# Tap matrices of a depthwise convolution: built in the feed-forward network before it and fetched back from DRAM, with the modulation steps of the two convolution stages redistributed

## The chip, the core and the metric

The kernel runs on one core of a Trainium2 chip. A core has a matrix engine (TensorE, PE in the profile; its weight loads are a row of their own, PEld), a vector engine (VectorE, DVE), a scalar engine (ScalarE, ACT), a general engine (GpSimd, POOL) and a sync engine (SyncE, SP) that here issues nearly all DMA transfers. Each engine works through its own instructions in their written order and waits on semaphores for the others.

The metric is the device time of one launch in microseconds. The kernel before takes 2255.34 us (median of three runs, 2252.38 to 2259.39).

## The reference

A trunk of two layers over 256 positions of 2048 channels, fp32, with one conditioning vector `c`:

```python
for i in range(2):
    mod = silu(c) @ ada_w[i] + ada_b[i]          # 6 x 2048 modulation values
    sh_m, sc_m, gt_m, sh_f, sc_f, gt_f = split(mod, 6)
    h = x * (1 + sc_m) + sh_m
    y = s5_mixer(h) if i == 0 else conv_mixer(h)
    x = layer_norm(ALPHA * x + (1 + gt_m) * y)
    h = x * (1 + sc_f) + sh_f
    x = layer_norm(ALPHA * x + (1 + gt_f) * swiglu_ffn(h))     # hidden width 5632

def conv_mixer(u):
    ab = u @ w_pw1                                # 2048 x 4096
    v = ab[..., :d] * sigmoid(ab[..., d:])
    v = depthwise_causal_conv(v, w_dw, 31 taps) + b_dw
    return silu(layer_norm(v)) @ w_pw2            # 2048 x 2048
```

## The kernel before, in words

**Stages.** The S5 mixer and its gated projection (to about 395 us of the span), the feed-forward network of layer 0 (FFN0, about 420 to 1152), an entry panel (1152 to 1179) that starts the first pointwise product of the convolution while the layer norm behind FFN0 is finished, that product with the depthwise convolution (to about 1390), the second pointwise product pw2 (to about 1490), and the feed-forward network of layer 1 (FFN1, to about 2235).

**Weights.** They are streamed from DRAM once, in units. A load of SP (line 586) brings a unit into a tile `raw`; ACT rounds it to `whi` (line 860), DVE forms the rest `wlo = raw - whi` (line 861, 128x2048 elements), and PE multiplies (lines 931 and 935): 16 matmuls with `whi` and 8 with `wlo` for a unit. FFN0 has two parts: in each, first panels of four units from `w_gu` (gate and up projections), then units from `w_down`. Within a panel the gated product is made by ACT and DVE from PSUM (`fsg`, lines 1286 to 1288), turned by PE (`turned`, line 947) and split for the down product (line 952). The first pointwise product of the convolution has the same form with `sg` (line 1134).

**Modulation.** Two thirds of `silu(c) @ ada_w`, most of layer 1's and some of layer 0's, are not done as matmuls but as a queue of 128 steps (`AdaQueue`). A step is a 1 MB load `rawa` on SP (line 687) and a multiply-add `adaacc` over 128x2048 on DVE (line 702). When the steps of a part are all done, four matmuls `adar` and four transposes `adat` on PE add it up. A step is drawn once for each weight unit whenever a credit that grows by `ada.rate` reaches one, and none while `ada.hold` is set.

**Convolution.** Of 16 chunks of 128 channels some have their 31 taps summed on DVE (line 1732, from `pad` or `vpad`), and eleven go over PE: POOL multiplies a mask `fold` with the taps into a matrix `lw` (line 1646, 128x1024, three buffers), the padded chunk goes to DRAM (`scr<-pad`) and comes back shifted (`vs<-scr`), and 32 matmuls `conv<-vs,lw` (line 1769, 32x256) give the sums. What runs later than the unit it is called in is put in a list `later` with a number of units.

**Order.** A scheduler fixes each engine's instruction order when the program is built; `queue_behind` holds an instruction behind another of the same engine.

## Time and profile before

| | |
|---|---|
| runs | 2252.38, 2255.34, 2259.39 us |
| profiled execution | 2254.45 us, of which the span is 2252.4 us |
| granted TensorE clock | 0.995 |
| PE busy in the span | 2200.4 us (98%) |
| DVE | 1677.5 us (74%) |
| ACT | 1017.3 us (45%) |
| POOL | 155.4 us (7%) |
| DMA | 579.50 MB, mean 257 GB/s |

The span runs from the first to the last instruction of the profiled execution; 2.05 us of its time lie outside the span. A timeline row gives the start in the span, the duration, the engine, the line, the operation with the tile written and the tiles read, and in brackets the idle time before it with what ended it. Rows of the same kind that follow one another are merged, with their count.

### The profile page before, as it was taken

Reading aid. Unit: us, or ns where it says so; the run is one execution under the profiler, and the core shown is the slowest. Engines: PE = TensorE matmul, PEld = TensorE weight load, DVE = VectorE, ACT = ScalarE, POOL = GpSimd, SP = SyncE. Lnnn points to the kernel's source line nnn. Section 1 sums busy time; section 2 is a strip of 40 time slices with the busy share of each in tenths; the row PEclk is TensorE's granted clock in tenths of the full one; section 3 lists DMA queues with packets and bytes.
Section 4 is the critical chain, followed back from the end, with each engine's and each line's share of the span. In section 5 each row is a group of like instructions: output and inputs, shape, how many; then the busy total and the mean of one; then the engine's idle time right before and its main releaser. Section 6 shows DMA issues by size and latency. Waiting matters only on the chain.

```text
span 2252.4 us, 33443 instructions
## 1 busy us (share of the span) xinstructions
PE 2200.4 (98%) x13619; PEld 1795.8 (80%) x13619; DVE 1677.5 (74%) x1839; ACT 1017.3 (45%) x1234; POOL 155.4 (7%) x265
## 2 busy tenths in 40 slices
PE   6999999999999999999999999999999999999998
PEld 4556778888787888787897777898888888888888
DVE  8897998887777777777988979888755444555474
ACT  4775334644333333344455434566434333434343
POOL 5771000000000000000010010000000000000000
PEclk9999999999999999999999999999999999999999
DMA  9998999599999899999856686757865555555542
GB/s 333 346 324 281 326 347 303 184 321 319 325 321 329 322 319 323 319 326 323 301 178 189 212 217 231 274 187 236 279 222 186 194 194 189 187 189 187 187 166 96
DMA packets 382848, 579.50 MB, mean 257 GB/s; under 512 B 13923, under 2 KB 282355, under 8 KB 368227
## 3 DMA queue, kind: packets, MB, share of 16 engines
q1 hardware_dynamic: 382070, 576.82, 75.5%
q8 instruction: 107, 1.75, 0.3%
q0 software_dynamic: 384, 0.46, 0.1%
q14 instruction: 47, 0.39, 0.1%
q10 hardware_dynamic: 240, 0.08, 0.0%
HBM read 573.74 MB, written 3.57 MB: 256 GB/s over the span
## 4 chain that ended last, share of the span: by engine, by line
PE 80%; DVE 10%; DMA 4%; ACT 2%; issue 2%; SPq 1%; POOL 0%; POOLq 0%; DVEq 0%; ACTq 0%
PE acc L931 65%; PE acc L935 8%; DVE wlo L861 2%; DMA raw<-in_ffn_w_gu_dram 2%; PE acc L1043 2%; PE turned L947 2%; PE conv L1769 2%; ACT whi L860 1%; DVE adaacc L702 1%; DMA raw<-in_s_w_glu_dram 1%; DMA raw<-in_ada_w_dram 1%; DVE pin L476 1%; PE ada L630 1%; PE y L499 1%; PE adar L710 0%
## 5 line engine op out<-in xcount | busy, mean ns | idle before, releaser
L861 DVE TENSOR_TENSOR wlo<-raw,whi 128x2048 fp32r<-128x2048 f32 x343 | 786.6, 2294 | 451.6 <-ACT whi L860 448.3
L860 ACT CAST whi<-raw 128x2048 fp32r<-128x2048 f32 x343 | 653.8, 1906 | 794.6 <-PE acc L931 424.5
L931 PE MATMUL acc<-whi,h 128*128 128x512 f32 x3584 | 873.7, 393 | 4.2 <-ACT whi L860 4.0
L931 PEld LDWEIGHTS acc<-whi,h 128*128 128x128 f32 x3584 | 667.3, 188 | 151.0 <-ACT whi L860 7.1
L931 PE MATMUL acc<-wlo,h 128*128 128x512 f32 x1792 | 453.6, 390 | 1.9 <-DVE wlo L861 1.8
L931 PEld LDWEIGHTS acc<-wlo,h 128*128 128x128 f32 x1792 | 335.4, 188 | 73.5 <-DVE wlo L861 4.2
L931 PE MATMUL acc<-whi,f 128*128 128x512 f32 x1248 | 300.9, 391 | 0.0
L702 DVE SCALAR_TENSOR_TENSOR adaacc<-rawa,c_act,adaacc 128x2048 f32<-128x2048 f32 (+1 forms) x135 | 284.6, 2108 | 0.4
L931 PEld LDWEIGHTS acc<-whi,f 128*128 128x128 f32 x1248 | 232.8, 188 | 49.5 <-ACT whi L860 1.7
L931 PE MATMUL acc<-wlo,f 128*128 128x512 f32 x624 | 156.6, 389 | 0.0
L931 PEld LDWEIGHTS acc<-wlo,f 128*128 128x128 f32 x624 | 117.0, 188 | 24.6 <-DVE wlo L861 0.4
L1646 POOL TENSOR_TENSOR lw<-fold,wtap 128x1024 f32<-128x1024 f32 x11 | 24.0, 2187 | 1050.5 <-PE acc L935 860.0
L935 PE MATMUL acc<-h,whi 128*128 128x256 f32 x640 | 83.7, 285 | 0.8 <-DVE h L1843 0.8
L935 PEld LDWEIGHTS acc<-h,whi 128*128 128x128 f32 x640 | 79.0, 191 | 6.1 <-issue 4.2
L630 PE MATMUL ada<-raw,c_rep 128*32 128x512 f32 (+1 forms) x576 | 69.2, 564 | 7.1 <-DMA raw<-in_ada_w_dram 6.9
L1286 ACT ACTIVATE fsg<-acc 128x256 f32<-128x256 f32 x84 | 31.7, 380 | 96.8 <-PE acc L931 96.8
L1224 POOL CAST lnmh<-lno 128x2 fp32r<-128x2 f32 x1 | 0.2, 183 | 874.2 <-DVE lno L68 874.2
L1287 DVE TENSOR_TENSOR fsg<-acc,fsg 128x256 f32<-128x256 f32 x84 | 35.1, 420 | 18.2 <-ACT fsg L1286 18.1
L935 PE MATMUL acc<-h,wlo 128*128 128x256 f32 x320 | 43.0, 283 | 0.0
L935 PE MATMUL acc<-f,whi 128*128 128x256 f32 x320 | 40.8, 284 | 0.0
L935 PEld LDWEIGHTS acc<-h,wlo 128*128 128x128 f32 x320 | 40.4, 192 | 0.0
L935 PEld LDWEIGHTS acc<-f,whi 128*128 128x128 f32 x320 | 39.4, 192 | 0.2
(367 smaller groups left out, 1837.8 us busy)
## 6 DMA issues: line engine op xcount, KB each, us to landing
raw<-in_ffn_w_gu_dram SPq DMA_DIRECT2D x352, 512.0 KB, 4.7
rawa<-in_ada_w_dram SPq DMA_DIRECT2D x128, 1024.0 KB, 5.6
raw<-in_ffn_w_down_dram SPq DMA_DIRECT2D x88, 1024.0 KB, 5.1
raw<-in_ada_w_dram SPq DMA_DIRECT2D x64, 1024.0 KB, 7.5
raw<-in_cv_w_pw_dram SPq DMA_DIRECT2D x66, 512.0 KB, 5.0
raw<-in_s_w_glu_dram SPq DMA_DIRECT2D x64, 512.0 KB, 10.2
raw<-in_cv_w_pw_dram SPq DMA_DIRECT2D x15, 1024.0 KB, 5.4
vs<-scr SPq DMA_DIRECT2D x40, 142.0 KB, 4.8
```

The costliest lines, as they stand in the source:

```text
L630: nc.tensor.matmul(acc[32 * (k % 4):32 * (k % 4) + 32, :], c_rep[:, kk, :], r[:, k, :], start=kk < 4, stop=kk >= NCH - 4)
L702: nc.vector.scalar_tensor_tensor(out=acc, in0=r[:, i], scalar=c_act[:, kk:kk + 1], in1=acc, op0=MUL, op1=ADD)
L860: m1 = nc.scalar.copy(out=hi[:, ks], in_=r[:, ks])
L861: m2 = nc.vector.tensor_tensor(out=lo[:, ks], in0=r[:, ks], in1=hi[:, ks].bitcast(F32), op=SUB)
L931: nc.tensor.matmul(acc[bank].rearrange("p a b -> p (a b)"), x[:, bank * HALF:(bank + 1) * HALF], wt[:, k], start=first, stop=end)
L935: nc.tensor.matmul(acc[bank][:, i], wt[:, k, m * P:(m + 1) * P], x, start=first and i == 0, stop=end and i == len(banks[bank]) - 1)
L947: nc.tensor.transpose(b[:, o:o + HALF], u[t][:, c0 + k * P:c0 + (k + 1) * P], ident)
L1043: nc.tensor.matmul(acc[m][:, 0:EW], wt[:, k, m * P:(m + 1) * P], xx[:, 4 * u + k], start=u == 0 and n == 0, stop=u == 3 and n == len(order ...
L1286: nc.scalar.activation(out=t[:, i], in_=gv[:, 0], func=AF.Sigmoid)
L1287: nc.vector.tensor_tensor(out=t[:, i], in0=gv[:, 0], in1=t[:, i], op=MUL)
L1646: nc.gpsimd.tensor_tensor(out=lw, in0=fold32.unsqueeze(1).unsqueeze(1).broadcast_to([P, 4, CONV_G, 32]), in1=bc(wtap[:, :, 4 * c:4 * c + 4 ...
L1769: nc.tensor.matmul(acc[32 * q:32 * q + 32, :], lw[:, q, g, :], vs[:, q, 4 * g:4 * g + SEQ], start=g == 0, stop=g == n - 1)
```

## The change

**Tap matrices.** A new `taps_matrix(c, h)` makes half a chunk's matrix (128x512) on POOL, into a tile that shares its two buffers with the tag `hf`, and SP writes it (256 KB) to a DRAM tile, `lw_kept[c]`. It is put into FFN0's list `later` at units 50 to 106, 22 times (eleven chunks, two halves). In the convolution the POOL operation (128x1024) goes, and `kept_taps(c)` loads the 512 KB of a chunk from DRAM into `lw`, ahead of the `vs<-scr` copies. The DRAM pool now lives as long as the kernel.

**Modulation steps.** `ada.rate` is 0.5 instead of 0.25 in the convolution, and `ada.hold` is no longer lifted for pw2. The convolution draws seven steps instead of two, pw2 none instead of five; 128 in all, as before.

```diff
         ada.rate, ada.behind = 0.77, True
+        dramp = ctx.enter_context(tc.tile_pool(name="dram", bufs=1, space=bass.MemoryType.DRAM))
+        lw_kept = {c: dramp.tile([P, 4, CONV_G * 32], F32, name=f"lw{c}") for c in range(NCH) if c not in V_CHUNKS or c == 15}
+
+        def taps_matrix(c, h):
+
+            t = sp.tile([P, 2, SEQ], F32, tag="hf", name="lw", bufs=2)
+            with queue_behind(newest.marks):
+                nc.gpsimd.tensor_tensor(
+                    out=t.rearrange("p q (g c) -> p q g c", c=32), in0=fold32.unsqueeze(1).unsqueeze(1).broadcast_to([P, 2, CONV_G, 32]),
+                    in1=bc(wtap[:, :, 4 * c + 2 * h:4 * c + 2 * h + 2].rearrange("p g q -> p q g"), 3, 32), op=MUL)
+            nc.sync.dma_start(lw_kept[c][:, 2 * h:2 * h + 2], t)
+
+        for n, c in enumerate(lw_kept):
+            for h in range(2):
+                later.put(50 + (27 * (2 * n + h)) // 10, lambda c=c, h=h: taps_matrix(c, h))
         entry = ffn(0, mod[0][:, 5], stats, wp, sp, fp, entry, (cv_w_pw1[0], [(0, 256), (D, 256)]),
...
-        dramp = cvctx.enter_context(tc.tile_pool(name="dram", bufs=1, space=bass.MemoryType.DRAM))
...
-        ada.rate = 0.25
+        ada.rate = 0.5
...
-        def taps_matrix(c):
+        def kept_taps(c):
             lw = cp.tile([P, 4, CONV_G, 32], F32, tag="lw", name="lw", bufs=3)
-            nc.gpsimd.tensor_tensor(
-                out=lw, in0=fold32.unsqueeze(1).unsqueeze(1).broadcast_to([P, 4, CONV_G, 32]),
-                in1=bc(wtap[:, :, 4 * c:4 * c + 4].rearrange("p g q -> p q g"), 3, 32), op=MUL)
+            nc.sync.dma_start(lw.rearrange("p q g c -> p q (g c)"), lw_kept[c])
             return lw
...
+            lws = []
+
+            def back():
+                lws.extend(kept_taps(ch + k) for k in range(len(vs)))
+                conv_copies(scr[i], vs)
+
             if i == 6:
                 to_scratch()
-                later.put(1, lambda: conv_copies(scr[i], vs))
+                later.put(1, back)
             else:
                 later.put(wait - 3, to_scratch)
-                later.put(wait - 2, lambda: conv_copies(scr[i], vs))
+                later.put(wait - 2, back)
             for k, v in enumerate(vs):
-                lw = taps_matrix(ch + k)
-                later.put(wait + k, lambda k=k, v=v, lw=lw: conv_out(ch + k, v, lw))
+                later.put(wait + k, lambda k=k, v=v: conv_out(ch + k, v, lws[k]))
...
-            v, lw = cp.tile([P, 4, LS], F32, tag="vs", name="vs", bufs=3), taps_matrix(c)
+            v, lw = cp.tile([P, 4, LS], F32, tag="vs", name="vs", bufs=3), kept_taps(c)
...
-        ada.hold = False
         ada.finish(1, 2)
         stats = Stats("ln10", sp)
-        ada.rate, ada.credit = 1.0, 0.0
...
             if q == 3:
-                ada.hold = True
                 raw = entry_raw(fp)
...
-            ada.rate = 0.5
```

**Where the instructions land.** SP's instructions at the seam of FFN0's first part, where its loads go over from `w_gu` to `w_down`. Before:

```order
127 L586 DMA raw<-in_ffn_w_gu_dram 128x4x256 x2
128 L586 DMA raw<-in_ffn_w_down_dram 128x4x512
129 L687 DMA rawa<-in_ada_w_dram 128x2048
130 L586 DMA raw<-in_ffn_w_down_dram 128x4x512
131 L687 DMA rawa<-in_ada_w_dram 128x2048
132 L586 DMA raw<-in_ffn_w_down_dram 128x4x512
133 L687 DMA rawa<-in_ada_w_dram 128x2048
134 L586 DMA raw<-in_ffn_w_down_dram 128x4x512 x2
```

The changed kernel at the same place (`lw_4597<-lw` is a write of half a matrix to DRAM):

```order
131 L586 DMA raw<-in_ffn_w_gu_dram 128x4x256 x2
132 L1623 DMA lw_4596<-lw 128x512
133 L1623 DMA lw_4597<-lw 128x512
134 L586 DMA raw<-in_ffn_w_down_dram 128x4x512
135 L1623 DMA lw_4597<-lw 128x512
136 L1623 DMA lw_4598<-lw 128x512
137 L687 DMA rawa<-in_ada_w_dram 128x2048
138 L1623 DMA lw_4598<-lw 128x512
139 L1623 DMA lw_4599<-lw 128x512
140 L586 DMA raw<-in_ffn_w_down_dram 128x4x512
141 L1623 DMA lw_4599<-lw 128x512
142 L1623 DMA lw_4600<-lw 128x512
```

Here 17 of the 22 writes follow one another in pairs, each pair ahead of one load (a `w_down` unit and a `rawa` by turns at first, the last ones all ahead of `w_down` units), and the sixth `w_down` load is the first with none ahead of it but a `rawa`; the other five stand some 100 instructions earlier, near the third panel of that part. Each write waits for its POOL operation, and each POOL operation for the write two before it.

PE's instructions in a panel of FFN0's second part. Before:

```order
677 L931 MATMUL acc<-whi,h 128x512 x16
678 L931 MATMUL acc<-wlo,h 128x512 x8
679 L947 MATMUL turned<-ident,fsg 128x128
680 L931 MATMUL acc<-whi,h 128x512 x5
681 L947 MATMUL turned<-ident,fsg 128x128 x3
```

The changed kernel:

```order
676 L931 MATMUL acc<-whi,h 128x512 x16
677 L931 MATMUL acc<-wlo,h 128x512 x8
678 L947 MATMUL turned<-ident,fsg 128x128
679 L931 MATMUL acc<-whi,h 128x512 x8
680 L947 MATMUL turned<-ident,fsg 128x128 x3
```

Eight matmuls instead of five stand between the first turn and the other three, in the five panels of that part whose turns are split so; in the last four panels of the first part it is six instead of five, and at the first part's seam, where one turn, five matmuls and three turns stood, all four turns now stand in one row.

DVE's instructions in the convolution, around the gate (`sg`) of one panel. Before:

```order
1012 L1134 TENSOR_TENSOR sg<-acc,sg 128x256
1013 L1732 SCALAR_TENSOR_TENSOR V<-vpad_9915,taps_10263,V 128x256
1014 L1732 SCALAR_TENSOR_TENSOR vacc<-vpad_9915,taps_10263,vacc 128x256
1015 L1732 SCALAR_TENSOR_TENSOR V<-vpad_9915,taps_10263,V 128x256
1016 L1732 SCALAR_TENSOR_TENSOR vacc<-vpad_9915,taps_10263,vacc 128x256
1017 L1732 SCALAR_TENSOR_TENSOR V<-vpad_9915,taps_10263,V 128x256
1018 L1732 SCALAR_TENSOR_TENSOR vacc<-vpad_9915,taps_10263,vacc 128x256
1019 L1732 SCALAR_TENSOR_TENSOR V<-vpad_9915,taps_10263,V 128x256
1020 L861 TENSOR_TENSOR wlo<-raw,whi 128x2048
1021 L1134 TENSOR_TENSOR sg<-acc,sg 128x256
```

The changed kernel:

```order
1007 L861 TENSOR_TENSOR wlo<-raw,whi 128x2048
1008 L1799 SCALAR_TENSOR_TENSOR V<-conv,vec,shift 128x128x2
1009 L702 SCALAR_TENSOR_TENSOR adaacc<-rawa,c_act,adaacc 128x2048
1010 L781 TENSOR_TENSOR cln_s<-V 128x512
1011 L786 TENSOR_TENSOR cln_s<-lnsq 128x512
1012 L1134 TENSOR_TENSOR sg<-acc,sg 128x256
1013 L861 TENSOR_TENSOR wlo<-raw,whi 128x2048
1014 L1134 TENSOR_TENSOR sg<-acc,sg 128x256
1015 L1749 SCALAR_TENSOR_TENSOR vacc<-vpad_9994,taps_10340,vacc 128x256
```

The second `sg` now stands ahead of the run of tap sums, and a modulation step's `adaacc` stands ahead of the first. On PE the 32 `conv` matmuls of a chunk move from the middle of a panel to its start, right behind the four `turned`, and `adar` and `adat` of one modulation part move from pw2 into the fifth panel.

## The prediction

> **What bounds the kernel now.** I read the page's busy shares and its chain first, then a table of stretches, then the timeline at each place where PE waits.
>
> ```profile
> PE 2200.4 (98%) x13619; PEld 1795.8 (80%) x13619; DVE 1677.5 (74%) x1839; ACT 1017.3 (45%) x1234; POOL 155.4 (7%) x265
> PE 80%; DVE 10%; DMA 4%; ACT 2%; issue 2%; SPq 1%; POOL 0%; POOLq 0%; DVEq 0%; ACTq 0%
> L1646 POOL TENSOR_TENSOR lw<-fold,wtap 128x1024 f32<-128x1024 f32 x11 | 24.0, 2187 | 1050.5 <-PE acc L935 860.0
> ```
>
> PE is busy 98% of the span, so only the short waits of PE can be won, and any new wait of PE is lost in full. POOL's 24.0 us in the convolution are not on the chain themselves.
>
> ```profile
> core 0: us, PE busy (x) PEld busy (x) DVE busy (x) ACT busy (x) POOL busy (x), PEclk, DMA share, GB/s
> 655.00:705.00 50.00, 49.53 (x226) 39.72 (x226) 37.25 (x24) 18.73 (x15) 0.00 (x0) 1.00 0.91 327
> 1250.00:1390.00 140.00, 136.27 (x1182) 104.19 (x1175) 126.00 (x203) 50.45 (x60) 13.49 (x6) 1.00 0.70 207
> ```
>
> The seam of FFN0's first part (655 to 705) has DMA engines busy 0.91 and DVE 37.25 of 50 us; the convolution has DVE busy 126 of 140 us and DMA 0.70. The clock is 1.00 throughout, so durations can be carried from one stage to another.
>
> **The change part by part.** *The taps leave the convolution.* What one POOL operation does to DVE shows in the entry panel (the chain of waits) and in the convolution (timeline):
>
> ```profile
> 1154.80 2.19 DVE h L1005
> 1157.07 2.03 DVE h L1005
> ```
>
> ```profile
> 1161.47 2.19 PE L1043 MATMUL acc<-h,wlo 128*128 128x258 f32 x16 [0.62 <-DVE wlo L861]
> 1166.43 1.13 PE L829 MATMUL lnrep<-lny,row_of 128*128 128x128 f32 x8 [0.73 <-DVE lny L76]
> 1252.52 2.33 POOL L1646 TENSOR_TENSOR lw<-fold,wtap 128x1024 f32<-128x1024 f32 x1 [14.02 <-PE conv L1769]
> 1252.54 0.47 DVE L1732 SCALAR_TENSOR_TENSOR vacc<-vpad,taps,vacc 128x256 f32<-128x256 f32 x1
> 1252.93 2.20 DVE L1732 SCALAR_TENSOR_TENSOR V<-vpad,taps,V 128x256 f32<-128x256 f32 x1
> ```
>
> A tap sum of 0.47 us takes 2.20 while POOL works, 1.73 more; the two `h` of the entry, of the same size, take 2.19 and 2.03, about 3.3 more together. Without them the `wlo` queued behind them starts over 3 us earlier, and PE's 0.62 is gone. The 0.73 before `lnrep` hangs on a chain of small DVE operations behind `wlo`; I take half of it. Gain 1.0 (0 to 1.35). Eleven such holds of at most 2.2 us fall away in the convolution and entry, and five `adaacc` come into the convolution.
>
> *Gates in the convolution.* PE waits there for `sg`:
>
> ```profile
> 1261.85 2.28 DVE L861 TENSOR_TENSOR wlo<-raw,whi 128x2048 fp32r<-128x2048 f32 x1
> 1264.52 0.55 PE L947 MATMUL turned<-ident,sg 128*128 128x128 f32 x3 [0.95 <-DVE sg L1134]
> 1292.10 0.55 PE L947 MATMUL turned<-ident,sg 128*128 128x128 f32 x3 [1.29 <-DVE sg L1134]
> ```
>
> The second `sg` stood behind seven tap sums and a `wlo`. It now stands before the tap sums. Of 0.95 + 1.29 = 2.24 us I take 1.8, and leave 0.4 for `adaacc` ahead of the first gate. Behind the gates the tap sums are late next; they feed only DVE's own later sums, and 126 of 140 us is still below full.
>
> *Steps out of pw2.* One of its five steps costs PE time:
>
> ```profile
> 1449.67 2.35 DVE L702 SCALAR_TENSOR_TENSOR adaacc<-rawa,c_act,adaacc 128x2048 f32<-128x2048 f32 x1
> 1455.55 4.49 DVE L861 TENSOR_TENSOR wlo<-raw,whi 128x2048 fp32r<-128x2048 f32 x2
> 1457.89 2.11 PE L931 MATMUL acc<-wlo,h 128*128 128x512 f32 x8 [1.79 <-DVE wlo L861]
> ```
>
> Without the 2.35 us of `adaacc` the `wlo` comes before PE asks: gain 1.8 (0 if the statistics behind it fill the place). In the convolution five steps are 5 x 2.35 = 11.8 us of DVE, which the eight holds that fall away there (8 x up to 1.73 = 13.8) make room for. The steps' places are new: pw2's one in five at 1.79 us bounds them from below at about 2, and two such in five from above at 4; the two steps already there cost nothing. I take 1.0. The eleven `lw` loads and five `rawa` add 5.5 + 5 MB to a stretch of 211 us at about 207 GB/s, some 44 MB: the share rises from 0.70 to about 0.87. SP orders them among the weights; their cover is the 13% left, and nothing if that is unevenly spread, which the same 0 to 4 holds.
>
> *The reordered turns in FFN0.* All five of PE's waits there, from the view of waits, and the larger ones:
>
> ```profile
> PE turned L947 <- DVE fsg L1288: 5.2, 5, 2.0
> ```
>
> ```profile
> 585.91 0.55 PE L947 MATMUL turned<-ident,fsg 128*128 128x128 f32 x3 [1.29 <-DVE fsg L1288]
> 610.37 0.55 PE L947 MATMUL turned<-ident,fsg 128*128 128x128 f32 x3 [1.95 <-DVE fsg L1288]
> 678.03 0.55 PE L947 MATMUL turned<-ident,fsg 128*128 128x128 f32 x3 [0.47 <-DVE fsg L1288]
> 905.87 0.55 PE L947 MATMUL turned<-ident,fsg 128*128 128x128 f32 x3 [0.97 <-DVE fsg L1288]
> 1447.77 2.88 PE L931 MATMUL acc<-whi,h 128*128 128x512 f32 x12
> 1450.49 1.98 PE L931 MATMUL acc<-wlo,h 128*128 128x512 f32 x8
> ```
>
> Twelve matmuls start to start take 1450.49 - 1447.77 = 2.72 us, 0.227 each, so a unit of 24 lasts 5.44. One more matmul ahead of the wait is worth 0.23 at 585.91 and at 610.37; three more are worth 0.68 at 905.87 and all of the fifth wait (5.2 less the four is 0.5). At the seam the gates now stand ahead of `wlo` and `adaacc`, so the 0.47 goes. Gain 2.1 (0 to 5.2).
>
> *Writes into FFN0.* The POOL work moves to where DVE has `wlo` and `adaacc` in hand, and the writes go past SP's loads. POOL's own price, its wait behind DVE, and the writes:
>
> ```profile
> L362 POOL TENSOR_TENSOR xq<-tq,wt 128x512 f32<-128x512 f32 x3 | 3.2, 1059 | 0.2
> 213.12 0.73 POOL L1423 TENSOR_TENSOR h<-gl,h 128x256 fp32r<-128x256 f32 x1 [11.34 <-ACT h L1422]
> 225.48 2.28 DVE L861 TENSOR_TENSOR wlo<-raw,whi 128x2048 fp32r<-128x2048 f32 x1
> 226.09 2.28 POOL L1423 TENSOR_TENSOR h<-gl,h 128x256 fp32r<-128x256 f32 x1 [12.23 <-ACT h L1422]
> ```
>
> ```profile
> raw<-in_ffn_w_down_dram SPq DMA_DIRECT2D x88, 1024.0 KB, 5.1
> out_dram<-X SPq DMA_DIRECT2D x8, 256.0 KB, 2.1
> scr<-pad SPq DMA_DIRECT2D x2, 287.0 KB, 3.9
> ```
>
> A half matrix costs POOL 1.06 us. If a `wlo` runs already, POOL waits for its end: 2.28 instead of 0.73, 1.55 lost. At the seam, with two buffers, a pair of writes can go only when the pair before has landed and two new halves are made, while SP stands still and the loads behind wait. The period of a pair is at least 2.1 + 2 x 1.06 = 4.2 us (quiet write, POOL undisturbed) and at most 3.9 + 2 x (1.06 + 1.55) = 9.1. I take 5.5: a landing of 2.6, nearer the quiet row, since SP lets only one 1 MB load out between two pairs, two operations, and one wait of half a `wlo` at DVE's three quarters, 0.8.
>
> ```profile
> 657.92 0.37 SPq L586 DMA_DIRECT2D raw<-in_ffn_w_down_dram  x1
> 665.73 0.37 SPq L586 DMA_DIRECT2D raw<-in_ffn_w_down_dram  x1
> 670.20 0.37 SPq L586 DMA_DIRECT2D raw<-in_ffn_w_down_dram  x1
> 677.67 4.21 SPq L586 DMA_DIRECT2D raw<-in_ffn_w_down_dram  x2
> 682.77 3.79 PE L931 MATMUL acc<-whi,f 128*128 128x512 f32 x16
> 682.77 1.91 ACT L860 CAST whi<-raw 128x2048 fp32r<-128x2048 f32 x1 [3.13 <-DMA raw<-in_ffn_w_down_dram]
> 689.29 3.93 PE L931 MATMUL acc<-whi,f 128*128 128x512 f32 x16
> ```
>
> SP reaches the first pair some 2 us before 657.92, at about 655.7, with its halves long made. The `w_down` loads then follow pairs 1, 3, 5, 7 and 8: the first keeps its time, the second goes at 655.7 + 2 x 5.5 = 666.7, the third at 677.7 (was 670.20), the fourth at 688.7 (was 677.67), the fifth at 694.2 (was 681.5). A load lands after 5.1 and is cast in 1.9. The third unit is then ready at 684.7 where PE asks at 682.77: 1.9 late. The fourth is ready at 695.7 against 689.29 + 1.9: 4.5 late. The fifth, 701.2, is in time, and the backlog is worked off behind it. Together 6.4; nothing at a period of 4.2 to 4.4, about 13 at 6.5, 28 at 9.1. Queued behind the waiting writes are also `rawa`, which only `adaacc` waits for. The first five writes, 20 us into the part, fall where SP has room, but up to three operations hold DVE for 1.06 each next to a gate: 1.5 (0 to 3.2).
>
> [...]
>
> **Sum**, against the profiled execution's 2254.45 (span 2252.4 and 2.05 around it): -1.0 - 1.8 - 1.8 - 2.1 = -6.7 won; +1.0 + 6.4 + 1.5 = +8.9 lost; +2.2. The median of the runs shown is 0.9 above that execution, so 2257 or so against 2255.34: no change, since about 0.3% (6.8 us) is what a measurement of this kernel can tell.
>
> **Rivals.** *One, the writes hide.* The pair period is at most 4.4 us: writes land as fast as at the quiet end and POOL finds gaps. For it: DVE idles 12.75 us of 50 and nothing but one load stands ahead of a pair. Against it: 0.91 of DMA busy, and the row at 226.09. The gains stay whole with 0 to 1 us lost: 2255.34 - 6.7 + 0.5, 2249, and 2247 if more of the turns' waits go; the bound of faster is 2248.6. Chance 0.18.
>
> *Two, SP stalls the seam.* The period is 6.2 us or more, at which the seam loses 11 and the sum passes +6.8, slower than before. For it: a landing of 3.9 with loads ahead alone gives 6.0 undisturbed, and both operations of a pair may wait. Against it: the held SP thins the loads, and while PE waits DVE has gaps. At a period of 6.5 the loss is 13: 2255.34 - 6.7 + 2.5 + 13 = 2264. Chance 0.23.
>
> *Three, DVE is the bound at the seam.* Seventeen operations hold DVE 17 x 1.06 = 18 us, in some 45 us where it has about 12 to spare. If each holds it in full, `wlo` and gates are 6 late on top: 2257 + 6 = 2263. For it: rows of 2.20 and 2.19. [...] Chance 0.05.
>
> *Four, the convolution fills.* With a DMA share of 0.87 and DVE at 0.9 each of five steps costs 1.79 instead of one: 9 us instead of 1.0, 2265. Chance 0.04; the falling holds speak against it.
>
> **How the numbers follow.** The forecast, no change at 2257, has 0.50; its own range is 2250 to 2262. Faster is rival one with 0.18, slower rivals two to four with 0.23 + 0.05 + 0.04 = 0.32. The range for 8 in 10 reaches from rival one's 2248 to rival two at 6.7 us of period, 2266.
>
> **What would show it.** At the seam, POOL rows of 1.06 to 2.6 us in pairs, 5 to 6 us apart, SP writes between single `w_down` loads, `whi` waiting for DMA and two waits of PE before units at about 683 and 691 of 2 and 4 us; if PE has none there, rival one holds, if they sum to over 11, rival two. In the entry panel `h` at 0.48 us and no wait of PE for `wlo`; in the convolution no DVE row of a tap sum over 0.5, at most 0.4 before `turned`; in pw2 no wait for `wlo` near 1455; in FFN0's second part waits before `turned` under 0.3. The forecast is wrong if the writes land far from 2.6 us, or if a step in the convolution finds PE asking.

## The result, and the profile after

| | before | changed |
|---|---|---|
| median of five runs each, measured side by side | 2257.80 us | 2292.77 us |
| lowest and highest of the changed kernel | | 2285.61, 2293.05 us |
| ratio (95% interval) | | 1.0152 (1.0134 to 1.0169) |
| profiled execution | 2254.45 us | 2292.79 us, span 2291.0 |
| granted TensorE clock | 0.995 | 0.989 |

The change makes the kernel 35 us slower. The forecast was no change at 2257 us with a range to 2266; slower by over 0.3% had a chance of 0.32, and no rival reached 2292.

Where the time went is read from PE. The same weight matmuls run in the same order in both kernels, so the position of the n-th of them in the one trace, less its position in the other, shows how late the changed kernel is there. What it gains or loses between two points (us, in the span of the kernel before) is this:

| to 425 | 425 to 470 | 470 to 655 | 655 to 735 | 735 to 1150 | 1150 to 1180 | 1180 to 1389 | 1389 to 1490 | to 2230 | sum |
|---|---|---|---|---|---|---|---|---|---|
| -1.0 | +6.4 | -1.9 | +17.4 | +4.2 | -1.3 | +18.3 | -3.8 | -0.2 | +38.2 |

The first column is scatter: the programs do not differ there, and in the runs below it lies between -1.1 and +4.1. All the loss is in four places: the first five halves near 450, the seam (655 to 735), the rest of FFN0, and the convolution (1180 to 1389). The entry panel and pw2 gain. The page's busy row and its chain, of the changed kernel:

```profile
PE 2217.4 (97%) x13619; PEld 1804.9 (79%) x13619; DVE 1671.1 (73%) x1839; ACT 1015.7 (44%) x1234; POOL 168.5 (7%) x276
PE 69%; DVE 14%; DMA 9%; ACT 4%; issue 2%; POOL 1%; SPq 0%; POOLq 0%; DVEq 0%; ACTq 0%
```

PE has the same 13619 matmuls and is busy 17 us longer. A large part of that is matmuls that run at a lower granted clock (column PEclk), and a table of stretches of the changed kernel shows where; in its second row the clock is full and PE simply waits:

```profile
core 0: us, PE busy (x) PEld busy (x) DVE busy (x) ACT busy (x) POOL busy (x), PEclk, DMA share, GB/s
450.00:465.00 15.00, 11.55 (x42) 9.17 (x41) 13.86 (x13) 8.62 (x10) 1.07 (x1) 0.77 0.83 283
675.00:690.00 15.00, 11.30 (x51) 8.84 (x49) 9.49 (x8) 2.49 (x3) 10.13 (x6) 1.00 0.84 272
690.00:710.00 20.00, 13.41 (x45) 9.75 (x46) 9.51 (x4) 4.28 (x3) 7.45 (x5) 0.74 0.90 294
1320.00:1335.00 15.00, 12.14 (x56) 9.27 (x46) 10.95 (x11) 8.54 (x9) 0.00 (x0) 0.77 0.54 181
1355.00:1375.00 20.00, 15.69 (x68) 12.08 (x60) 18.21 (x29) 4.48 (x4) 0.00 (x0) 0.91 0.60 168
```

**The seam.** The timeline of SP (writes of halves are L1623, the next weights L586) and then that of PE:

```profile
659.33 0.97 SPq L1623 DMA_DIRECT2D lw<-lw  x2
661.05 0.38 SPq L586 DMA_DIRECT2D raw<-in_ffn_w_down_dram  x1
667.54 1.37 SPq L1623 DMA_DIRECT2D lw<-lw  x2
671.68 3.41 SPq L1623 DMA_DIRECT2D lw<-lw  x2
675.18 0.39 SPq L586 DMA_DIRECT2D raw<-in_ffn_w_down_dram  x1
677.85 1.37 SPq L1623 DMA_DIRECT2D lw<-lw  x2
682.82 3.41 SPq L1623 DMA_DIRECT2D lw<-lw  x2
686.31 0.39 SPq L586 DMA_DIRECT2D raw<-in_ffn_w_down_dram  x1
...
706.29 0.32 SPq L1623 DMA_DIRECT2D lw<-lw  x1
```

```profile
682.56 3.92 PE L931 MATMUL acc<-whi,f 128*128 128x512 f32 x16 [1.99 <-ACT whi L860]
686.32 1.98 PE L931 MATMUL acc<-wlo,f 128*128 128x512 f32 x8
693.62 6.17 PE L931 MATMUL acc<-whi,f 128*128 128x512 f32 x16 [5.33 <-ACT whi L860]
699.63 1.98 PE L931 MATMUL acc<-wlo,f 128*128 128x512 f32 x8
705.58 5.38 PE L931 MATMUL acc<-whi,f 128*128 128x512 f32 x16 [2.98 <-ACT whi L860]
...
719.66 2.56 PE L931 MATMUL acc<-whi,f 128*128 128x512 f32 x10 [0.95 <-ACT whi L860]
```

From 659.33 to 706.29 eight pairs go by, 5.87 us each. PE waits 1.99 + 5.33 + 2.98 + 0.95 = 11.25 us for `whi`, and the sixteen matmuls behind the second and third wait last 6.17 and 5.38 us instead of 3.79 (the prediction's row at 682.77), 4.0 us more. The kernel before waits 0.5 us there. Some 2 to 3 of the 17.4 us are left: a wait of 0.56 us for `yt` at 726.18, and small delays of matmuls that I did not follow further. The halves and their writes, from the groups and the DMA issues (KB and median us to landing):

```profile
L1620 POOL TENSOR_TENSOR lw<-fold,wtap 128x512 f32<-128x512 f32 x22 | 36.2, 1656 | 378.7 <-DMA lw<-lw 236.9 <-DVE h L952 141.4 <-POOL lw L1620 0.2
```

```profile
lw<-lw SPq DMA_DIRECT2D x22, 256.0 KB, 3.9
lw<-lw SPq DMA_DIRECT2D x11, 512.0 KB, 6.6
```

A half takes POOL 1.66 us on average, not 1.06, and a write lands after 3.9 us in the median, not 2.6.

**Near 450.** POOL's first halves stand ahead of two gates. Toward the end of POOL's row from 443.12 to 449.4 two small operations of DVE take 1.30 us each, and 0.47 after it; PE waits 3.45 us for a gate, and the eight `wlo` matmuls behind take 3.76 us instead of 1.98 (the prediction's row at 1450.49):

```profile
443.12 6.30 POOL L1620 TENSOR_TENSOR lw<-fold,wtap 128x512 f32<-128x512 f32 x2 [2.88 <-DMA lw<-lw]
447.17 1.30 DVE L1277 SCALAR_TENSOR_TENSOR sg<-sg,ecol 128x256 f32<-128x256 f32 x1
448.40 1.30 DVE L1276 TENSOR_TENSOR sg<-sg,h 128x256 f32<-128x256 f32 x1
...
450.83 0.47 DVE L1277 SCALAR_TENSOR_TENSOR sg<-sg,ecol 128x256 f32<-128x256 f32 x1
```

```profile
453.73 0.47 PE L947 MATMUL turned<-ident,fsg 128*128 128x128 f32 x1 [3.45 <-DVE fsg L1288]
...
454.92 3.76 PE L931 MATMUL acc<-wlo,h 128*128 128x512 f32 x8
```

**The convolution.** PE's longest waits there, with what ACT and DVE did ahead of them:

```profile
1321.34 0.64 ACT L1761 COPY V<-conv 128x256 f32<-128x256 f32 x1 [3.31 <-DVE conv L1756]
1321.78 1.90 ACT L860 CAST whi<-raw 128x2048 fp32r<-128x2048 f32 x1
1323.74 6.80 PE L931 MATMUL acc<-whi,h 128*128 128x512 f32 x16 [2.86 <-ACT whi L860]
```

```profile
1351.41 3.70 ACT L860 CAST whi<-raw 128x2048 fp32r<-128x2048 f32 x2
1361.12 0.46 DVE L1749 SCALAR_TENSOR_TENSOR V<-vpad,taps,V 128x256 f32<-128x256 f32 x1
1361.50 2.28 DVE L861 TENSOR_TENSOR wlo<-raw,whi 128x2048 fp32r<-128x2048 f32 x1
1363.83 3.61 PE L931 MATMUL acc<-wlo,h 128*128 128x512 f32 x8 [4.31 <-DVE wlo L861]
```

The two `whi` were made from 1351.41 to 1355.1, but `wlo` starts at 1361.50: in DVE's order it stands behind a run of over 20 tap sums (mostly L1749) that began at 1351.57. The wait at 1323.74 has a like history: ACT's cast at 1321.78 stood behind a copy that needed the end of another such run. Both waits end in matmuls at half rate. Of the 18.3 us, 9.0 are waits of PE (11.9 against 2.9 in the kernel before), about 4 the half rate behind them, 1.9 the convolution's own matmuls, which take longer in their new places, and 1.4 matmuls that come over from pw2 (below).

**What was won.** In the entry panel `h` is back at its undisturbed length, and no wait for `wlo` is left. pw2's wait for `wlo` near 1455 is gone, and the convolution's gates wait for nothing:

```profile
1158.56 0.47 DVE L1005 SCALAR_TENSOR_TENSOR h<-X,m1g,h 128x256 fp32r<-128x256 f32 x1
...
1163.15 0.48 DVE L1005 SCALAR_TENSOR_TENSOR h<-X,m1g,h 128x256 fp32r<-128x256 f32 x1
```

```profile
1260.09 0.66 PE L947 MATMUL turned<-ident,sg 128*128 128x128 f32 x4
1287.89 0.60 PE L947 MATMUL turned<-ident,sg 128*128 128x128 f32 x4
```

### The profile page after: what moved, and what is told of

Read it like the earlier page. It is cut to its first block, busy times and chain, and to the rows that moved or that the text cites. A ratio compares the mean times of both kernels' runs of the same rounds, so it can differ in the third digit from the quotient of the medians.

```text
span 2291.0 us, 33504 instructions
## 1 busy us (share of the span) xinstructions
PE 2217.4 (97%) x13619; PEld 1804.9 (79%) x13619; DVE 1671.1 (73%) x1839; ACT 1015.7 (44%) x1234; POOL 168.5 (7%) x276
## 4 chain that ended last, share of the span: by engine, by line
PE 69%; DVE 14%; DMA 9%; ACT 4%; issue 2%; POOL 1%; SPq 0%; POOLq 0%; DVEq 0%; ACTq 0%
PE acc L931 55%; PE acc L935 7%; DMA raw<-in_ffn_w_gu_dram 4%; DVE wlo L861 4%; ACT whi L860 2%; DMA raw<-in_ffn_w_down_dram 2%; DVE adaacc L702 2%; PE acc L1043 1%; PE turned L947 1%; DMA lw<-lw 1%; DVE vacc L1749 1%; DVE V L1749 1%; DMA raw<-in_s_w_glu_dram 1%; PE ada L630 1%; DVE pin L476 1%
## 5 line engine op out<-in xcount | busy, mean ns | idle before, releaser
L1620 POOL TENSOR_TENSOR lw<-fold,wtap 128x512 f32<-128x512 f32 x22 | 36.2, 1656 | 378.7 <-DMA lw<-lw 236.9
L1786 PE MATMUL conv<-vs,lw 128*32 128x256 f32 x672 | 40.4, 381 | 2.5 <-ACT vs L1781 2.5
```

What stands on the lines that cost most here:

```text
L1620: nc.gpsimd.tensor_tensor(out=t.rearrange("p q (g c) -> p q g c", c=32), in0=fold32.unsqueeze(1).unsqueeze(1).broadcast_to([P, 2, CONV_G, ...
L1786: nc.tensor.matmul(acc[32 * q:32 * q + 32, :], lw[:, q, g, :], vs[:, q, 4 * g:4 * g + SEQ], start=g == 0, stop=g == n - 1)
```

## The experiments

The first theory after the result was this: SP's standstill behind the pairs of writes makes the loss of FFN0, and the five steps, which bring their loads and DVE work into the convolution, make the loss there. Its rivals: the written bytes alone (22 times 256 KB, 5.8 MB) in FFN0; and for the convolution the tap matrices' loads, the order in which the scheduler puts tap sums or convolution matmuls among the weights, or the buffers that the steps take. For each run a line of a table of the same kind stands below its text; "FFN0" is 425 to 1150, with near 450, seam (655 to 735) and the rest of it apart where that matters. Each ratio is to the kernel before on the same chip.

### One edit at a time

`e1_steps_only` is the kernel before with the modulation edit; `e2_taps_only` is the change without it.

```diff
-        ada.rate = 0.25
+        ada.rate = 0.5
...
-        ada.hold = False
         ada.finish(1, 2)
         stats = Stats("ln10", sp)
-        ada.rate, ada.credit = 1.0, 0.0
...
             if q == 3:
-                ada.hold = True
                 raw = entry_raw(fp)
...
-            ada.rate = 0.5
```

This is e1 against the kernel before; e2 has the same lines the other way round, against the changed kernel.

> The kernel before with the modulation edit alone: seven steps in the convolution, none in pw2; the tap matrices are made by POOL in the convolution as before. Theory A (the steps rearrange DVE's order in the convolution: tap sums stand in runs of up to 22 ahead of the wlo that PE waits for): slower than before by 11 to 17 us, lost between 1230 and 1390 us of the span, with PE waits of 3 us or more there and 2 to 4 us won back in pw2. Rival B (the convolution is slowed by the eleven lw loads among its weights): within 3 us of before or faster.

> The change with the modulation edit undone (two steps in the convolution, five in pw2): matrices made in FFN0, written, and loaded in the convolution. Theory A: slower by 19 to 25 us, all of it in FFN0 (about 6 near 450, 15 at the seam, 3 in the second part), the convolution no slower than before. Rival B (lw loads): slower by 35 us or more, with 12 or more of it in the convolution.

| | median | ratio | 425 to 470 | seam | 735 to 1150 | entry | convolution | pw2 |
|---|---|---|---|---|---|---|---|---|
| e1_steps_only | 2262.91 | 1.0033 (1.0017 to 1.0048) | 0.0 | -0.3 | +0.9 | 0.0 | +8.7 | -3.7 |
| e2_taps_only | 2273.73 | 1.0077 (1.0062 to 1.0092) | +5.2 | +13.2 | +2.0 | -1.4 | -2.2 | +1.6 |

The steps alone cost the convolution 8.7 us and win 3.7 in pw2. The tap matrices alone cost FFN0 some 20 us and win 2.2 in the convolution, where their loads then stand in SP's queue without harm. That e2 is 1.6 us slower in pw2 is no loss of its own: the same wait of 1.79 us as before is followed by matmuls at half rate there (last section). The convolution's 18.3 is not the sum of +8.7 and -2.2: the two edits hurt each other there by some 12 us.

### FFN0: standstill or bytes

`e3_taps_spread` is e2 with the halves in a list of their own. `ada.finish`, called ahead of each part's down product, empties the list `later`, and that is what puts 17 of the 22 halves at the seam; the new list is not emptied. Each write is also held behind the newest weight load, so that one goes every two or three units.

```diff
-    later, turning = Later(), Later()
+    later, turning, making = Later(), Later(), Later()
...
+            making.tick()
...
-            nc.sync.dma_start(lw_kept[c][:, 2 * h:2 * h + 2], t)
+            with queue_behind(loads):
+                nc.sync.dma_start(lw_kept[c][:, 2 * h:2 * h + 2], t)
...
-                later.put(50 + (27 * (2 * n + h)) // 10, lambda c=c, h=h: taps_matrix(c, h))
+                making.put(50 + (27 * (2 * n + h)) // 10, lambda c=c, h=h: taps_matrix(c, h))
```

> As the run before, but the 22 halves come from a list of their own that is not emptied at the seam, and each write is issued behind the newest weight load, so that one write stands every two to three units over FFN0 instead of 17 at the seam. The same POOL work, the same bytes. Theory A (the writes cost because they stand together and two buffers make SP wait): FFN0 within 2 us of before, the whole -4 to +2. Rival C (each write or each POOL operation costs by itself, through DVE's holds or DMA traffic): half or more of the loss stays, +10 or more.

Four more runs start from the kernel before and add only part of what the change puts into FFN0; nothing in the convolution uses what they write. Two write at the seam: `f1_clump_nopool` writes 22 times 256 KB from a tile that is ready (four writes for each of the units from 46 on, held behind the newest load), without POOL work; `f2_clump_tiny` has the change's POOL work and SP places, and writes 16 KB each time. `f3_spread_nopool` and `f4_spread_tiny` do the same with e3's spread places.

The write of f1 and f3, which have no POOL operation, and then that of f2 and f4, each against the write of the change:

```diff
-            nc.sync.dma_start(lw_kept[c][:, 2 * h:2 * h + 2], t)
+            nc.sync.dma_start(lw_kept[c][:, 2 * h:2 * h + 2], c_rep.rearrange("p a b -> p (a b)").rearrange("p (q n) -> p q n", q=2))
```

```diff
-            nc.sync.dma_start(lw_kept[c][:, 2 * h:2 * h + 2], t)
+            nc.sync.dma_start(lw_kept[c][:, 2 * h:2 * h + 2, 0:16], t[:, :, 0:16])
```

> The kernel before, with the 22 writes of 256 KB put at the seam of FFN0's first part, four behind each load, from a tile that is ready (no POOL work, so SP never stands still for a buffer; the written data are not used, the convolution makes its matrices as before). Theory A (SP stands still between pairs because two buffers must land and be made again): at the seam at most 4 us lost, nothing near 450. Theory E (5.8 MB more in a stretch where the DMA engines are 0.9 busy): 8 us or more lost between 650 and 740.

> The kernel before, with the change's 22 POOL operations and writes at the change's places, but only 16 KB of each half written (hardly any bytes; the written data are not used). Theory A: SP's standstill stays, with a shorter landing: a period of 4.5 to 5 us and 2 to 8 us lost at the seam, and the 5 us near 450 stay, being POOL's hold on DVE. Theory E: under 2 us at the seam.

> The kernel before, with 22 writes of 256 KB spread over FFN0 (one behind every second or third load), from a ready tile, without POOL work; the data are not used. The run with spread halves lost 8 us in FFN0. If the bytes are the cause (theory E): 5 to 9 us lost there again. If POOL's hold on DVE is the cause (theory F): 2 or less.

> The kernel before, with 22 POOL operations spread over FFN0 as in the run with spread halves, but only 16 KB of each half written; the data are not used. Theory E: 2 us or less lost in FFN0. Theory F: 5 to 9 us lost.

| | median | ratio | 425 to 470 | 470 to 655 | seam | 735 to 1150 |
|---|---|---|---|---|---|---|
| e3_taps_spread | 2263.12 | 1.0027 (1.0014 to 1.0039) | +0.3 | +1.9 | -0.2 | +6.2 |
| f1_clump_nopool | 2269.06 | 1.0055 (1.0040 to 1.0070) | 0.0 | +0.9 | +9.7 | +2.8 |
| f2_clump_tiny | 2272.74 | 1.0062 (1.0045 to 1.0079) | +4.8 | -2.2 | +12.8 | +2.3 |
| f3_spread_nopool | 2261.15 | 1.0023 (1.0010 to 1.0037) | 0.0 | +0.1 | +0.9 | +8.2 |
| f4_spread_tiny | 2259.40 | 1.0014 (1.0003 to 1.0026) | +0.3 | -0.7 | +0.3 | +3.5 |

Neither theory holds alone. With next to no bytes SP's standstill costs the seam 12.8 us, more than was expected of it; without the standstill the 22 writes of f1 cost 9.7, where the standstill theory allowed 4 at most. Not all of the 9.7 need be bytes, since four writes of f1 also keep SP's queue busy for 2.2 to 3.6 us. The sum, 22.5, is above the 17.4 and 13.2 of the change and of e2, so the two costs overlap. Near 450 it is POOL's work (f2 +4.8, f1 nothing). In f2 the pairs go from 660.86 to 697.68 in seven periods of 5.3 us, though only 16 KB are written: such a write still lands after 3.0 us in the median, so the period hangs little on the bytes. PE's waits there:

```profile
683.20 3.93 PE L931 MATMUL acc<-whi,f 128*128 128x512 f32 x16 [1.77 <-ACT whi L860]
691.37 5.52 PE L931 MATMUL acc<-whi,f 128*128 128x512 f32 x16 [2.43 <-ACT whi L860]
703.45 6.22 PE L931 MATMUL acc<-whi,f 128*128 128x512 f32 x16 [3.75 <-ACT whi L860]
```

Spread out, the writes do not become free: f3 loses 8.2 us after 735, where the DMA engines are fullest. The stretch 800 to 1020 in the kernel before, and then in f3:

```profile
800.00:1020.00 220.00, 218.41 (x991) 177.61 (x989) 170.05 (x121) 85.87 (x68) 0.00 (x0) 1.00 0.92 319
```

```profile
800.00:1020.00 220.00, 215.26 (x969) 173.70 (x968) 167.80 (x118) 85.62 (x67) 0.00 (x0) 1.00 0.95 331
```

FFN0 streams at 319 GB/s with 0.92 of the engines' time before anything is written; 331 at 0.95 is what f3 moves with the writes, and 22 fewer matmuls are done in the stretch. So f3's writes do not all find room beside the weights there. How much of the 8.2 is bytes and how much the writes' places in SP's queue was not separated: f4, with 16 KB a write at the same places and POOL's work, loses 3.5 after 735. These figures are of one profile each and differ by some 6 us for the same spread halves: 6.2 after 735 in e3, 9.6 to 11.9 in the runs g1, g2 and k3 below.

### The convolution: what in the steps costs

`e4_steps_behind` is e1 with the tap sums held behind the newest `wlo` of DVE, which cuts their runs from up to 20 to at most 8 in the middle of the stretch. `k1_steps_pehold` is e1 with the convolution's matmuls held behind PE's newest weight matmul, which puts them back where the kernel before has them (e1 has them one or two units earlier). `k2_steps_pehold_behind` has both.

The hold of the tap sums (e4, k2), and that of the convolution's matmuls (k1, k2):

```diff
-        def conv_taps(ch, acc, z, js, begin, last):
+        def conv_taps(*args):
+            with queue_behind(newest.marks):
+                sum_taps(*args)
...
```

```diff
-            conv_groups(acc, vs, lw, CONV_G)
+            with queue_behind(newest_mm):
+                conv_groups(acc, vs, lw, CONV_G)
```

> The modulation edit alone, as in the first run, but each group of tap sums on DVE is queued behind the newest wlo, so that no more than about nine stand between two wlo. Theory A: the loss of the first run goes, -5 to +2 against before. If the five steps' DVE time or their loads are the cause (rival D), 8 us or more of loss stays.

> The modulation edit alone, with each chunk's 32 conv matmuls queued on PE behind the weight matmuls traced before them, which puts them back to the place that they have in the kernel before (behind two units of a panel instead of ahead of them). Loads, buffers and DVE work of the seven steps stay. Theory P (the loss of 9 us in the convolution comes from the conv matmuls' place, where PE needs the next weights at once after them): at most 3 lost in the convolution, the whole -3 to +2. Rival B2 (the 5 MB of rawa loads delay the weights): 6 to 9 lost there.

> As the run before, with each group of tap sums queued behind the newest wlo as well, so that DVE's runs are short. Theory P: the convolution loses no more than the run before does, and 2 us less if runs of tap sums cost there too; the whole -5 to 0. Rival B2: 6 to 9 lost in the convolution.

Three others take parts of a step away. `h1_steps_light` is e1 with a step of the convolution adding only 64 of its columns on DVE, its load still 1 MB; `l1_steps_small` cuts the load to these columns as well (both leave out that part of the modulation sums). `h2_slots_only` is the kernel before with five blanks in the convolution that take a `raw` buffer each, load 32 KB and do next to nothing.

The DVE part of h1 and l1, the load of l1, and the blanks of h2:

```diff
+            m = 64 if self.light else n
...
-                    nc.vector.scalar_tensor_tensor(out=acc, in0=r[:, i], scalar=c_act[:, kk:kk + 1], in1=acc, op0=MUL, op1=ADD)
+                    nc.vector.scalar_tensor_tensor(out=acc[:, :m], in0=r[:, i, :m], scalar=c_act[:, kk:kk + 1], in1=acc[:, :m], op0=MUL, op1=ADD)
```

```diff
             nc.sync.dma_start(
-                r, ada_w[layer, k * rows * P:(k + 1) * rows * P, j * D + 512 * b0:(j + 1) * D].rearrange("(k p) n -> p k n", p=P))
+                r[:, :, :m], ada_w[layer, k * rows * P:(k + 1) * rows * P, j * D + 512 * b0:j * D + 512 * b0 + m].rearrange("(k p) n -> p k n", p=P))
```

```diff
+            if self.blanks and self.blanks.pop(0):
+                r = rawp.tile([P, 4, 512], F32, tag="raw", name="rawa")
+                nc.sync.dma_start(r[:, 0, :64], ada_w[1, 0:P, 0:64])
...
```

> The modulation edit alone, with the DVE work of the convolution's steps cut to 64 of 2048 columns (part of the modulation sums is left out); the rawa loads and their buffers stay. With the edit alone the convolution lost 9 us (1180 to 1390). Theory S (each rawa takes one of the four raw buffers, so the weights are loaded later): 5 to 9 us lost there again. Rival V (the 2.35 us of DVE for each step): 2 us or less.

> The kernel before (two steps in the convolution, five in pw2), with five blanks added in the convolution: each takes a raw buffer, loads 32 KB into it and has DVE read four columns. Theory S: 4 to 9 us lost in the convolution. Rival V, or the bytes of rawa: 1 us or less.

> The modulation edit alone, with the convolution's steps cut in both their transfer and their DVE work: a step there loads and adds 64 of its columns only, so its load is at most an eighth of 1 MB; that part of the modulation sums is left out. The slots of the raw buffers and the order stay as in the edit alone. With DVE cut alone the stretch from 1180 to 1389 was 7.2 us longer than before, with everything 8.7, and with five small blanks in place of the five extra steps 1.2. If the 1 MB loads are the cost: +1 to +2 there. If the taking of buffers and the new order of PE are: still +6 or more. pw2 -3 to -4 in both.

| | median | ratio | convolution | pw2 |
|---|---|---|---|---|
| e1_steps_only (above) | 2262.91 | 1.0033 (1.0017 to 1.0048) | +8.7 | -3.7 |
| e4_steps_behind | 2262.79 | 1.0025 (1.0014 to 1.0036) | +9.8 | -3.7 |
| k1_steps_pehold | 2263.76 | 1.0021 (1.0008 to 1.0034) | +10.3 | -3.7 |
| k2_steps_pehold_behind | 2263.36 | 1.0035 (1.0017 to 1.0054) | +8.8 | -3.7 |
| h1_steps_light | 2259.38 | 1.0013 (1.0000 to 1.0025) | +7.2 | -3.7 |
| l1_steps_small | 2257.65 | 0.9999 (0.9986 to 1.0012) | +3.9 | -3.7 |
| h2_slots_only | 2268.00 | 1.0053 (1.0036 to 1.0069) | +1.2 | 0.0 |

With the steps alone, no order of tap sums or matmuls brings the 8.7 us back. In k2 the waits for `wlo` (3.8 us in e1) and the 1.9 us by which e1's convolution matmuls are longer are gone, but PE waits 6.0 for `whi` instead of 0.5 and pays some 2.5 of half rate, which e1 does not have.

By the profiles DVE's time is 1.5 of the 8.7 (e1 to h1) and the transfers another 3.3 (h1 to l1). Of the 3.9 left, 1.4 are no loss but the matmuls that add up a part of the modulation (`adar`, `adat`): they move from pw2 into the convolution, so pw2's -3.7 is 2.3 won and 1.4 moved. l1 was expected at +1 to +2. Of its rest of 2.5 some 1.4 are half rate behind a wait of 2.77 us for a gate at 1298.91; the kernel before has the gate's wait at 1.29 and no half rate. So the transfers are worth more than 3.3, by up to those 1.4. In l1 the smaller transfers also changed the order that the scheduler makes; k2 shows that holding the order wins nothing by itself. The buffers alone cost 1.2 (h2). The median of l1 is that of the kernel before, with part of the modulation left out.

h2's own time, 11.1 us over the kernel before, lies mostly elsewhere (+5.3 in FFN1, where PE does not wait but a quarter of its matmuls start 0.232 to 0.235 us apart instead of 0.227; +4.1 ahead of 425) and stays open.

What the transfers do shows in ACT's waits from 1195 to 1400, total, times and longest, in the kernel before and in e1:

```profile
ACT whi L860 <- DMA raw<-in_cv_w_pw_dram: 1.4, 1, 1.4
```

```profile
ACT whi L860 <- DMA raw<-in_cv_w_pw_dram: 20.4, 5, 7.3
```

A step's load takes one of the four `raw` buffers and 1 MB of SP's queue among weights of 512 KB, and five weights come late in e1. The DMA engines are not full there: their mean share from 1200 to 1390 is 0.72 in the kernel before, 0.75 in e1, 0.73 in the changed kernel, and 0.80 in e2, which loses nothing. So a lack of bandwidth on the mean is not the cause. Whether it is the loads' place in SP's queue or a lack of bandwidth for some microseconds was not separated for the steps.

### The convolution: both edits together

`g1_after_spread` is the whole change with e3's spread halves. `g2_after_spread_poolq` is g1 with the tap matrices' loads issued by POOL instead of SP (below). `k3_after_spread_pehold` is g1 with k1's hold of the convolution's matmuls.

```diff
-            nc.sync.dma_start(lw.rearrange("p q g c -> p q (g c)"), lw_kept[c])
+            nc.gpsimd.dma_start(lw.rearrange("p q g c -> p q (g c)"), lw_kept[c])
```

> The whole change with the halves spread over FFN0 as in the run with spread halves. There FFN0 lost 8 us, and the modulation edit alone lost 9 in the convolution and won 4 in pw2; the change lost 18 in the convolution. If the other 9 to 12 come from the lw loads standing among the weights of a convolution that is short of buffers (theory S): the convolution loses 15 to 20 again, the whole is 18 to 24 us slower. If they come from what FFN0 leaves behind: the convolution loses 5 to 9, the whole 8 to 13.

> As the run before, but the lw loads are issued by POOL's queue, which has nothing else to do there, instead of standing in SP's. If their place in SP's queue is what costs: the convolution loses 5 to 9. If their bytes cost: 12 or more.

> The whole change with spread halves (18 us lost in the convolution) and the conv matmuls held to their old place; the lw loads stay in SP's queue. If the 12 us that the lw loads in SP's queue cost come from the conv matmuls' place too (they need their matrices earlier): 5 or less lost in the convolution, the whole about +8. If SP's order alone costs: 12 to 18.

The last two start from the change itself. `l2_after_small_steps` has l1's cut of the steps (64 columns loaded and added). Its smaller transfers also gave PE and DVE nearly the order of the kernel before, with unbroken runs of at most 13 tap sums in the middle where the change has 18, 21 and 23, so `m1_after_held_orders` holds both orders (k2's edit) and leaves every transfer whole.

> The whole change with the convolution's steps cut in the same way (64 columns loaded and added; that part of the modulation sums is left out). FFN0 stays as in the change, about +24 to +28 by the end of it. Convolution, 1180 to 1389: the change lost 18.3. If the 1 MB step loads among the tap matrices' loads in SP's queue are the cause: -2 to +2 and 2275 in all. If the tap matrices' loads alone, or the taking of buffers, push the weights behind: +8 or more, 2283 or above.

> The whole change with both of the convolution's orders held near those of the kernel before, all transfers at full size: its conv matmuls behind the newest weight matmul of PE, its tap sums behind the newest wlo of DVE (runs of at most 8 tap sums in the middle of the stretch, where the change has 21 and 23). When the steps' transfers and DVE work were cut in the change, the stretch from 1180 to 1389 lost 0.8 instead of 18.3, but with smaller transfers the order of PE and DVE went back to nearly that of before as well. If the order is the cause: +1 to +4 there, 2275 to 2278 in all. If the 5 MB of step loads among the tap matrices' loads are: +12 or more, 2285 or above. In between: both, in the share that is measured. FFN0 as in the change, +24 to +28 by its end.

| | median | ratio | 425 to 470 | seam | 735 to 1150 | entry | convolution | pw2 |
|---|---|---|---|---|---|---|---|---|
| g1_after_spread | 2278.48 | 1.0102 (1.0087 to 1.0118) | +0.3 | +5.8 | +9.7 | -1.4 | +17.8 | -3.7 |
| g2_after_spread_poolq | 2264.48 | 1.0035 (1.0021 to 1.0048) | +0.3 | +0.3 | +11.9 | -1.4 | +5.4 | -3.7 |
| k3_after_spread_pehold | 2272.80 | 1.0073 (1.0047 to 1.0099) | +0.3 | -0.2 | +9.6 | -1.4 | +15.4 | -3.7 |
| l2_after_small_steps | 2272.41 | 1.0072 (1.0056 to 1.0088) | +2.9 | +14.5 | +3.2 | -1.4 | +0.8 | -3.8 |
| m1_after_held_orders | 2287.61 | 1.0130 (1.0109 to 1.0151) | +4.6 | +18.9 | +2.9 | -1.4 | +8.8 | -3.7 |

Without the steps' bytes and DVE work the convolution loses 0.8 instead of 18.3, and with the two orders held and the bytes whole it loses 8.8. So by these profiles 9.5 of the 18.3 hang on the order that comes with the change, whose runs of tap sums hold back `wlo` at 1361.50 and `whi` at 1321.78, and 8.0 on the steps' transfers and DVE time, as in e1. The medians bear out less of the 9.5: m1 is 30.2 us above the kernel before and the change 35.0, with some 1 us more lost in m1's FFN0. e1 has runs of up to 20 as well, and there holding them wins nothing (k2); why they cost something in the change, with the tap matrices' loads in the queue, is not shown by a run of its own. With both orders held m1 and k2 lose the same, 8.8 us each, with 6.2 and 6.0 us of waits for `whi` and some 2.5 of half rate: so held, the tap matrices' loads add nothing to what the steps cost. In m1 the convolution has two waits of PE left, both for weights, the first with its half rate behind it:

```profile
1269.94 6.72 PE L931 MATMUL acc<-whi,h 128*128 128x512 f32 x16 [3.64 <-ACT whi L860]
1355.56 3.92 PE L931 MATMUL acc<-whi,h 128*128 128x512 f32 x16 [2.54 <-ACT whi L860]
```

The place of the convolution's matmuls alone is not it: k3 keeps 15.4 of g1's 17.8, and what disappears before the convolution's matmuls comes back before the weights. g2 shows the third way out. With the tap matrices in POOL's queue the runs of tap sums are e1's, and the loss is 5.4, against 8.7 in e1. Most of the 3.3 between them is PE's waits for `wlo`, 1.5 us instead of 3.8: in e1 POOL still makes the matrices there and holds up a `wlo`, 3.81 us instead of 2.28:

```profile
1283.07 1.98 POOL L1646 TENSOR_TENSOR lw<-fold,wtap 128x1024 f32<-128x1024 f32 x1 [24.97 <-PE conv L1769]
1283.38 3.81 DVE L861 TENSOR_TENSOR wlo<-raw,whi 128x2048 fp32r<-128x2048 f32 x1 [1.43 <-ACT whi L860]
```

The runs themselves scatter as well: k3's lie between 2265.61 and 2283.80 us, and its profile is of the slowest; its place in the table is the least sure. The 5.8 us of g1 at the seam stand in one profile; k3 and g2 have the same FFN0 and lose nothing there.

Spreading, holding and POOL's queue all help, but no version was faster than the kernel before. The best versions that use the tap matrices and do all of the work, e3 and g2, are 0.3% slower than it.

## Why the prediction was wrong, point by point

| term | predicted | measured |
|---|---|---|
| entry panel | -1.0 | -1.3 |
| gates in the convolution | -1.8 | -2.1 |
| steps out of pw2 | -1.8 | -2.3, and 1.4 moved |
| reordered turns in FFN0 | -2.1 | about 0 |
| steps and loads in the convolution | +1.0 (0 to 4) | +19.0 |
| seam | +6.4 (0 to 28) | +17.4 |
| clump near 450 | +1.5 (0 to 3.2) | +6.4 |
| bytes written in FFN0 | none | see below |

**Entry, gates, pw2: right.** All three went where and about as far as predicted. In the convolution PE's time in the turns falls from 4.9 to 2.8 us; 18.3 + 2.1 - 1.4 = 19.0 is then what the steps and loads cost.

**Turns in FFN0: right in the first part, wrong in the second.** From 470 to 655 PE's two waits of 3.2 us become one of 1.2. From 800 to 1160 they grow instead; total, times and longest before, and then of the changed kernel:

```profile
PE turned L947 <- DVE fsg L1288: 1.4, 2, 1.0
```

```profile
PE turned L947 <- DVE fsg L1288: 3.7, 5, 1.4
```

None was to be over 0.3. The step "one more matmul ahead of the wait is worth 0.23" took the gate's own time as fixed; where PE reached its turns earlier the gates did not come earlier with it. What made them late was not tried.

**The seam: the mechanism was right, its size was not.** SP stood still between pairs, single `w_down` loads went between them, and the period of 5.87 us is near the 5.5. The landing was 3.9 instead of 2.6 and a half took 1.66 us. Rival two had both among its reasons. By the prediction's own points, 6.4 at 5.5 and 13 at 6.5, 5.87 gives 8.8 us of waits; 11.25 were measured. Part of the difference is that the first period alone is 8.2 us (659.33 to 667.54), where the delay was worked out with equal periods. By the prediction's own sign, waits that sum to over 11, rival two held, if all four are counted. What has no place in the sum is the half rate behind the two longer waits, 4.0 us. The writes without any standstill are a further cost that the sum does not have: f1 loses 9.7 us at the seam with SP never waiting for a half. Rival three, DVE as the bound, is a small part: from 655 to 710 its large operations are longer by 7 x 0.34 + 5 x 0.49, some 5 us (2.29 and 2.34 before), where that rival had 18, for a hold over each POOL operation's whole length, which was not shown:

```profile
L861 DVE TENSOR_TENSOR wlo<-raw,whi 128x2048 fp32r<-128x2048 f32 x7 | 18.4, 2629 | 21.5 <-ACT whi L860 21.4
L702 DVE SCALAR_TENSOR_TENSOR adaacc<-rawa,c_act,adaacc 128x2048 f32<-128x2048 f32 x5 | 14.2, 2835 | 0.0
```

**Near 450: a bound that was none.** "Up to three operations hold DVE for 1.06 each" gave 3.2 at most. Two operations of POOL last 6.30 us together there, and two small DVE operations ahead of the gate are held one after the other, the L1277 row at 1.30 instead of 0.47 and the L1276 row at 1.30 instead of 0.41. The one wait of 3.45 us that follows brings the half rate with it.

**The convolution: the failed step.** The price of five steps was taken from pw2's rows (one in five at 1.79) and from "the two steps already there cost nothing". That is a price of DVE time, and DVE time is the small part, 1.5 us in e1 to h1. A step also takes a quarter of the weights' buffers and twice a weight's bytes in SP's queue. The 13% that a mean DMA share of 0.87 left free were taken as cover, with "nothing if that is unevenly spread", and the price of that case was put into the same 0 to 4. The share measured from 1200 to 1390 was only 0.73, and the weights came late all the same. The prediction's own sign for this, a step that finds PE asking, came true. Rival four, the stretch filling up, had the right place and a chance of 0.04. That its 9 us lie near the 8.7 of e1 is luck: it is pw2's DVE price times five, for a stretch that fills up, and the stretch did not fill. Against it the falling holds of POOL were counted, and the convolution without them gains 2.2 (e2), all of it waits at the gates. Beyond rival four, the edits were priced one by one: the runs of over 20 tap sums ahead of a `wlo` stand in the order of DVE, and no term of the sum looked at them. In the change they cost up to 9.5 (m1).

**What the writes cost as bytes** was put at nothing apart from SP's stall. FFN0 was at 0.91 to 0.92 of DMA time, and the rows said so. f3 gives a price without POOL and without a standstill: 9.2 us from 425 to 1150 in its profile, about half of the 17.4 us that 5.8 MB take at 331 GB/s, and 5.8 between the medians.

So the forecast took each of the three losses from the low part of its range, and the ranges held only waits, without the half rate behind them. The measured seam lies inside its range; the convolution and the place near 450 lie outside theirs.

## What to carry to other kernels

FFN0's DMA engines were at 0.92 from 800 to 1020 and had little free room: 22 writes of 256 KB cost 6 to 9 us even when spread over FFN0 (f3, medians and profile). The work that they replaced, 24 us of POOL, was on no path and cost the convolution 2.2 us and the entry panel 1.4 (e2). A step that moves between stages has to be priced by all that it takes, its buffer and its place in the load queue before its engine time, and edits that meet in one stage by the instruction order that they give together. And a wait can cost more than its own length: behind five of the changed kernel's waits of PE, of 2.86 to 5.33 us, matmuls at half rate cost 1.6 to 3.0 us more.
